# Differential attention scores as one 128-row product, with the high and low parts split before the transposes

## The chip, the cores and the metric

The kernel runs on one core of one Trainium2 chip. The metric is device time in microseconds of one execution. Three runs of the kernel before took 1465.68 us at the median (1465.53 to 1467.9).

## The reference, cut to what matters

Two layers work on 256 latent tokens and 256 context tokens of 1024 channels. In each layer a normalised and modulated stream `h` is projected to the queries, keys and values of four attention branches (2-D neighbourhood "na", differential "df", grouped query "gq", latent "ml"). Each branch's output goes through its own projection, is weighted by a sigmoid gate and added up; an output projection and a gated MLP follow. In layer 0 the context tokens do all of this too; in layer 1 they give only keys and values.

The differential branch has 4 heads with 2 maps each of 32 channels, so 8 groups of 32 for the queries and 8 for the keys. It normalises each group (RMS and a gain), rotates the latent tokens' groups, and computes

```
sc = einsum("bqhmd,bthmd->bhmqt", q, k) * scale      # d = 32, 8 products per token pair
pr = softmax(sc)
a  = pr[:, :, 0] - lam * pr[:, :, 1]
o  = einsum("bhqt,bthd->bqhd", a, v)
```

## The kernel before, in words

All products of the large matrices are done in a rounded 32-bit format (`F32R`) with both operands split into a high and a low part, `x = hi + lo`: `hi*hi + lo*hi + hi*lo`, three matmuls (`mm3`, lines 277 to 280). Weights arrive on SyncE's queue into one of four raw tiles (`wload`, line 267), ScalarE writes the high part and VectorE the low one.

A layer first makes na's keys and values, then its queries. After that come four stages, each given to `drive` (line 282), which emits the steps of several generators in turn, in proportion to the weight that stands beside each. The stage of na's attention carries the projection of df's keys, values and queries; the stage of df's attention carries the gate product of na (`merge`) and gq's projection; and so on for gq and ml. The tile framework then puts the instructions of each engine into an order of its own by a simulated timeline, so an instruction can stand far from where the code emits it. Each engine runs its own list in that order, and semaphores hold what must wait.

A projection (`win_block`, line 442) works on halves of 256 tokens. For a query or key half, `use_qk` (line 636) copies the result from PSUM, normalises it, lets GpSimd rotate it if the tokens are latent, and puts one step `put` on a list, `later`, from which `due` takes one step at a time.

For branches in `SPLIT` (df in layer 0; na, df and gq in layer 1) `put` calls `to_ST` (line 600). It does four 128x128 transposes into one PSUM tile `tp`, and then for each of the four 32-row groups of df a ScalarE copy that rounds to the high part (for queries a second copy of it into another 32 rows) and a VectorE subtraction for the low part. So a key half takes 4 ScalarE and 4 VectorE instructions of 32 rows by 512, a query half 8 and 4. In context halves the gain is applied in these instructions. The result has, per group, 64 rows of the key tile with the high and the low part, 64 rows of the query tile with the high part twice, and the query's low part in a third place. df has 7 such halves: keys and queries of both token sets in layer 0 (4), keys of both and queries of the latent tokens in layer 1 (3).

The score of one map for 128 queries is then two matmuls (`head_scores`, lines 768 and 769): 64 rows for `q_hi*(k_hi + k_lo)` and 32 rows for `q_lo*k_hi`. There are 48 df scores: 16 with 512 keys and 16 with 256 in layer 0, 16 with 512 in layer 1. The same two lines serve na and gq in layer 1, with 128 and 64 rows there. After them `softmax` (line 772) runs on VectorE and ScalarE, and the probabilities are transposed (line 827) and multiplied with the values (line 835).

Keys and queries lie in tiles `kT` (or `kS`) and `qT` (or `qS`); na and gq share one buffer and df and ml another. ml's two small weight matrices and its two intermediate tiles lie in a pool of their own, `mp`. `mla_weights` (line 665) puts their two DMAs on SyncE's queue. `stage()` (line 577) gives a staging tile from a pool of three.

Of the kernel before, what the change touches and what calls it, by code (L numbers as in the profile page):

```python
# [10 lines left out]
F32 = mybir.dt.float32  # L11
F32R = mybir.dt.float32r
AF = mybir.ActivationFunctionType
ALU = mybir.AluOpType
# [217 lines left out]
def backbone(ctx: ExitStack, tc, wb, xT, cc, cb, sm, rg, bias, cst, out):  # L232
# [17 lines left out]
    def spool(es, name, bufs, **k):  # L250
        return es.enter_context(tc.tile_pool(name=name, bufs=bufs, reuse_waits="tile", **k))
# [230 lines left out]
    for l in range(L):  # L482
# [34 lines left out]
        yes = ExitStack()  # L517
        aes = ExitStack()
        qp = spool(aes, f"q{l}", 2)
        stp = spool(aes, f"st{l}", 3)  # L520
        rp = spool(aes, f"rp{l}", 1)


# [16 lines left out]
        kT, qT, Vt = {}, {}, {}  # L540

        split = SPLIT[l]
        nbig = 2 if "na" in split else 1

        def newkq(key):

            if nbig == 1 and key in ("na", "gq"):
                kT[key] = qp.tile([P, 2, T], F32, name="kT", bufs=1)
                qT[key] = qp.tile([P, 2, TT], F32, name="qT", bufs=1)
            else:  # L550
                kT[key] = qp.tile([P, 4, T], F32, name="kS", bufs=nbig)
                qT[key] = qp.tile([P, 6, TT], F32, name="qS", bufs=nbig)
            if key in split:
                kT[key], qT[key] = kT[key].bitcast(F32R), qT[key].bitcast(F32R)
            if key == "ml":
                for i in range(2):
                    kT["ml%d" % i], qT["ml%d" % i] = kT["ml"][:, 2 * i:2 * i + 2], qT["ml"][:, 2 * i:2 * i + 2]

# [41 lines left out]
        def to_ST(dst, src, scale, d, isq):  # L600
# [9 lines left out]
            for r in range(P // d):  # L610
# [10 lines left out]
                else:  # L621
                    stt(lo, tp[rs], g, hi[rs].bitcast(F32), ALU.mult, ALU.subtract)

        def cols(j):
            return slice(256 * j, 256 * j + 256)

        def tcols(t0, na):
            return slice(P * t0, P * (t0 + na))
# [7 lines left out]
        def use_qk(dst, key, h, d, mul, add, gain, tab=None, which=None, e=A):  # L636

            def f(t0, na, ps):
                n = h * d
                st = stage()[:, :na, :n]  # L640
                A.copy(st, ps[:, :, :n])
                r = head_rstd((v4(st, h), mul, add))
                tt(V, v4(st, h), v4(st, h), bc4(r, na, h, d), ALU.mult)
                g = gain
                if tab is not None and t0 < 2:
                    s2 = stage()[:, :na, :n]
                    rope(v4(s2, h), v4(st, h), tab, which, t0)
                    st, g = s2, None
                z = dst[key][:, :, tcols(t0, na)]

                def put():
                    if key in split:
                        to_ST((z[:, :4], z[:, 4:6]) if dst is qT else (z,), st, g, d, dst is qT)
                    else:
                        to_T(z[:, :n // P], st, g, e)
                return [put]
            return f
# [5 lines left out]
        mw = {}  # L663

        def mla_weights():
            mw["kv"] = mp.tile([P, 512], F32, name="wkv")
            nc.sync.dma_start(out=mw["kv"], in_=wb[l, KIDX["kvb",], :, :512])
            mw["q"] = mp.tile([P, 2, 384], F32, name="wq")
            nc.sync.dma_start(out=mw["q"][:96], in_=wb[l, KIDX["qb",], :96, :768].rearrange("p (k n) -> p k n", k=2))

        def use_mkv(t0, na, ps):
            st = stage()
            A.copy(st[:, :, 0:160], ps[:, :, 0:160])
            a, krn = st[:, :, 0:128], st[:, :, 128:160]
            r = head_rstd((a.unsqueeze(2), 1.0 / 128, EPS), (krn.unsqueeze(2), 1.0 / 32, EPS))
            tt(V, a, a, r[:, 0:2].unsqueeze(2).to_broadcast([P, 2, 128]), ALU.mult)
            tt(V, krn, krn, r[:, 2:4].unsqueeze(2).to_broadcast([P, 2, 32]), ALU.mult)
            if t0 < 2:
                rope(st[:, :, 160:192].unsqueeze(2), krn.unsqueeze(2), 1, 2, t0)
                krn = st[:, :, 160:192]  # L680
            got = {}

            def put():
                got["ma"] = mp.tile([P, 256], F32, name="mkv")
                to_T(got["ma"].unsqueeze(1), st[:, :, 0:128], vec("kvag"), A)

            def tok(t):
                ma = got["ma"]
                kv = acc_p.tile([P, 512], F32, name="acc")
                mm(kv, lhsT=ma[:, t * P:(t + 1) * P], rhs=mw["kv"], start=True, stop=True)  # L690
                kv4 = kv.rearrange("p (h d) -> p h d", h=4)
                A.copy(Vt["ml"][:, t0 + t].rearrange("p (h d) -> p h d", h=4), kv4[:, :, 64:128])
                skv = stage().rearrange("p a n -> p (a n)")[:, :384].rearrange("p (h d) -> p h d", h=4)
                kn = skv[:, :, 0:64]
                A.copy(kn, kv4[:, :, 0:64])
                r = head_rstd((kn.unsqueeze(1), 1.0 / 64, EPS))
                tt(V, kn, kn, r.unsqueeze(2).to_broadcast([P, 4, 64]), ALU.mult)
                G.tensor_copy(skv[:, :, 64:96], krn[:, t].unsqueeze(1).to_broadcast([P, 4, 32]))
                got[t] = lambda: mla_T(kT, skv, t0 + t, vec("mkc" if t0 else "mkx", 0, 96), A)

            return [put, lambda: tok(0), lambda: tok(1), lambda: got[0](), lambda: got[1]()]
# [8 lines left out]
        def use_mqa(t0, na, ps):  # L710
# [6 lines left out]
            def put():  # L717
                tp = tp_p.tile([P, 4, P], F32, name="tp")
                for i in range(2):
                    for a in range(2):  # L720
                        nc.tensor.transpose(tp[:96, 2 * i + a], st[:, a, 96 * i:96 * i + 96], ident)
                got["ma"] = mp.tile([P, 2, 256], F32, name="mqa")
                for i in range(2):
                    A.mul(got["ma"][:96, i], tp[:96, 2 * i:2 * i + 2].rearrange("p a t -> p (a t)"), vec("qag", i, 96))

# [31 lines left out]
        def head_scores(key, qs, qt, d, i, r, ik):  # L757
# [4 lines left out]
            n = T if qs == 0 else CL  # L762
            sps = sc_p.tile([P, T], F32, name="sc")
            c = qs * S + qt * P
            ro = r // 2 * 2 * d
            rs, r1 = slice(ro, ro + 2 * d), slice(r * d, r * d + d)
            kk = k[:, 2 * ik + r % 2, T - n:]
# [177 lines left out]
        rt = lay.tile([P, 2, 2, 2, RW], F32, name="rt", bufs=1)  # L945
        rgt = tmp.tile([P, 4, RW], F32, name="t")
        nc.sync.dma_start(out=rgt, in_=rg[l].rearrange("p (a w) -> p a w", a=4))
        rtab0 = tmp.tile([P, 2, 2, RW], F32, name="t")
        nc.sync.dma_start(out=rtab0, in_=cst[:, 512:].rearrange("p (a q w) -> p a q w", a=2, q=2))
        for j in range(2):  # L950
# [9 lines left out]
        y = yp.tile([P, KD, TT], F32, name="y")  # L960
        pp = spool(aes, f"p{l}", 3)
        ptp = spool(aes, f"pt{l}", 3)
        mp = spool(aes, f"mp{l}", 1)
        use_nk = use_qk(kT, "na", 4, 64, *b64, gna)
        for t in range(4):
            p3 = kv[t].rearrange("p (a n) -> p a n", a=1)
# [10 lines left out]
        drive((attend(PAIR, probs_na, Vt["na"], lambda h: 64 * h, post_plain(O)), na),  # L977
              (chain(win_block(l, "dk", A2, use_qk(kT, "df", 8, 32, *b32, vec("dgk"), 1, 1)),
                     win_block(l, "dv", A2, use_v("df")),
                     win_block(l, "dq", qh, use_qk(qT, "df", 8, 32, *q32, vec("dgq"), 0, 1)), flush()), 12 + nq),  # L980
              *early(3))
        newV("gq"); newkq("gq")
        O1 = newO()
# [201 lines left out]
```

## Time and profile before

| | |
|---|---|
| median of three runs | 1465.68 us |
| profiled execution, own time | 1467.0 us |
| its span | 1465.2 us |
| TensorE busy (matmul) | 1424.0 us, 97% |
| TensorE busy (weight load) | 1193.7 us, 81% |
| VectorE busy | 1053.9 us, 72% |
| ScalarE busy | 665.6 us, 45% |
| GpSimd busy | 203.8 us, 14% |

A row for a matmul gives its start and how long it was in flight. Matmuls are pipelined, so the flights of neighbours overlap, and what a matmul occupies of the engine is read from the distance between starts, not from its duration.

### The profile page before, as it was taken

To read this page: it belongs to the slowest core of one execution; us is meant where nothing else is said; L and a number is where in the kernel's file an instruction comes from. 1 tells how busy PE (TensorE), PEld (TensorE's weight loads), DVE (VectorE), ACT (ScalarE), POOL (GpSimd) and SP (SyncE) were. 2 spreads that over 40 slices of the span, in tenths; PEclk is the share of its full clock that TensorE was granted. 3 is DMA by queue.
4 is the path that set the end of the run, shared out by engine and by line. 5 is a ranking of instruction groups with operands and counts; after the bars stand their busy time and mean duration, and the time that the engine had idled before them with its cause. 6 is when DMAs were issued, how large, how long until landed. Compare 5 with 4: busy or idle time off the path is not lost.

```text
span 1465.2 us, 22330 instructions
## 1 busy us (share of the span) xinstructions
PE 1424.0 (97%) x8526; PEld 1193.7 (81%) x8526; DVE 1053.9 (72%) x1911; ACT 665.6 (45%) x1197; POOL 203.8 (14%) x191
## 2 busy tenths in 40 slices
PE   6999999999999998999999999999999999899999
PEld 3787777777677888888888888898788889899999
DVE  5688676747776547899999653778767575787884
ACT  5445543435333334543244432465646554564662
POOL 0253001223111200000000000043123321000000
PEclk9999999999999999999999999999999999999999
DMA  9522121213233541455797322233223343455553
GB/s 376 195 89 92 44 90 58 94 44 130 82 120 113 189 158 58 158 187 188 224 323 256 116 81 92 94 125 98 82 96 104 106 144 131 137 184 183 188 177 112
DMA packets 57930, 202.19 MB, mean 138 GB/s; under 512 B 6560, under 2 KB 8096, under 8 KB 57184
## 3 DMA queue, kind: packets, MB, share of 16 engines
q1 hardware_dynamic: 57824, 200.77, 40.5%
q8 instruction: 67, 1.10, 0.3%
q14 instruction: 39, 0.32, 0.1%
HBM read 199.69 MB, written 1.05 MB: 137 GB/s over the span
## 4 chain that ended last, share of the span: by engine, by line
PE 93%; issue 2%; DVE 2%; ACT 2%; DMA 1%; POOL 0%; SPq 0%; POOLq 0%; DVEq 0%; ACTq 0%
PE acc L278 26%; PE acc L280 26%; PE acc L279 25%; PE av L835 3%; PE sc L754 3%; PE tp L827 2%; PE sc L769 2%; PE sc L768 2%; DVE wl L257 1%; PE acc L730 1%; DMA mraw<-in_wb_dram 1%; ACT wh L272 1%; PE acc L690 1%; PE tp L372 0%; PE tp L608 0%
## 5 line engine op out<-in xcount | busy, mean ns | idle before, releaser
L272 ACT CAST wh<-raw 128x1024 fp32r<-128x1024 f32 (+1 forms) x272 | 279.6, 1029 | 465.8 <-PE acc L279 381.3
L278 PE MATMUL acc<-hh,wh 128*128 128x256 f32 (+1 forms) x1248 | 422.9, 340 | 7.9 <-ACT hh L424 3.9
L257 DVE TENSOR_TENSOR wl<-raw,wh 128x1024 fp32r<-128x1024 f32 (+1 forms) x272 | 332.3, 1222 | 129.0 <-ACT wh L272 123.3
L280 PE MATMUL acc<-hh,wl 128*128 128x256 f32 (+1 forms) x1248 | 417.9, 335 | 0.0
L279 PE MATMUL acc<-hl,wh 128*128 128x256 f32 (+1 forms) x1248 | 417.2, 335 | 0.0
L278 PEld LDWEIGHTS acc<-hh,wh 128*128 128x128 f32 x1248 | 237.7, 191 | 37.0 <-ACT hh L424 7.0
L280 PEld LDWEIGHTS acc<-hh,wl 128*128 128x128 f32 x1248 | 238.3, 191 | 26.2 <-issue 3.8
L279 PEld LDWEIGHTS acc<-hl,wh 128*128 128x128 f32 x1248 | 238.4, 191 | 25.6 <-issue 3.3
L257 POOL TENSOR_TENSOR r<-v,mhalf 128x4 f32<-128x4 f32 (+3 forms) x59 | 80.9, 1376 | 732.6 <-DVE v L405 450.5
L350 DVE SCALAR_TENSOR_TENSOR junk<-raw,cact 128x1024 bf16<-128x1024 f32 x128 | 157.1, 1227 | 17.0 <-DMA raw<-in_wb_dram 16.4
L278 PE MATMUL acc<-wh,hh 128*128 128x256 f32 (+3 forms) x496 | 149.5, 301 | 5.8 <-ACT hh L424 5.8
L279 PE MATMUL acc<-wl,hh 128*128 128x256 f32 (+3 forms) x496 | 147.5, 297 | 0.0
L280 PE MATMUL acc<-wh,hl 128*128 128x256 f32 (+3 forms) x496 | 145.9, 300 | 0.1
L279 PE MATMUL acc<-al,wh 128*128 128x256 f32 (+1 forms) x370 | 121.5, 328 | 0.0
L278 PE MATMUL acc<-ah,wh 128*128 128x256 f32 (+1 forms) x370 | 121.5, 328 | 0.0
L280 PE MATMUL acc<-ah,wl 128*128 128x256 f32 (+1 forms) x370 | 121.4, 328 | 0.0
L254 DVE SCALAR_TENSOR_TENSOR u<-acc,smt,u 128x255 f32<-128x255 f32 (+1 forms) x184 | 108.9, 594 | 4.1 <-ACT u L1084 2.9
L278 PEld LDWEIGHTS acc<-wh,hh 128*128 128x128 f32 x496 | 95.2, 192 | 15.1 <-ACT hh L424 8.3
L777 ACT ACTIVATE p<-sc,nm 128x512 f32<-128x512 f32 (+1 forms) x120 | 74.2, 619 | 66.9 <-DVE nm L774 39.1
L280 PEld LDWEIGHTS acc<-wh,hl 128*128 128x128 f32 x496 | 95.0, 192 | 9.4 <-issue 4.7
L279 PEld LDWEIGHTS acc<-wl,hh 128*128 128x128 f32 x496 | 95.3, 192 | 6.5 <-issue 4.1
L774 DVE TENSOR_REDUCE nm<-sc 128x1 f32<-128x512 f32 (+1 forms) x120 | 71.1, 598 | 36.5 <-PE sc L769 25.9
(165 smaller groups left out, 2065.7 us busy)
## 6 DMA issues: line engine op xcount, KB each, us to landing
raw<-in_wb_dram SPq DMA_DIRECT2D x328, 512.0 KB, 3.4
mraw<-in_wb_dram SPq DMA_DIRECT2D x16, 512.0 KB, 10.2
raw<-in_wb_dram SPq DMA_DIRECT2D x20, 384.0 KB, 2.9
x<-in_xT_dram SPq DMA_DIRECT2D x2, 1024.0 KB, 6.3
bt<-in_bias_dram SPq DMA_DIRECT2D x8, 256.0 KB, 2.9
xt<-in_xT_dram SPq DMA_DIRECT2D x2, 1024.0 KB, 6.9
raw<-in_wb_dram SPq DMA_DIRECT2D x4, 320.0 KB, 2.8
cact<-in_cb_dram SPq DMA_DIRECT2D x1, 1024.0 KB, 11.4
```

What stands on the lines that cost most here:

```text
L254: return V.scalar_tensor_tensor(out=out, in0=in0, scalar=scalar, in1=in1, op0=op0, op1=op1)
L257: e.tensor_tensor(out=out, in0=a, in1=b, op=op)
L272: A.copy(h[:, :w], r[:, :w])
L278: mm(ps, lhsT=a[0], rhs=b[0], start=first, stop=False)
L279: mm(ps, lhsT=a[0], rhs=b[1], start=False, stop=False)
L280: mm(ps, lhsT=a[1], rhs=b[0], start=False, stop=last)
L350: V.scalar_tensor_tensor(out=junk, in0=r, scalar=1.0, in1=cact[:, st_], op0=ALU.mult, op1=ALU.mult, accum_out=o)
L754: mm(sps[:, :n], lhsT=q[o:o + d, c:c + P], rhs=k[o:o + d, T - n:], start=True, stop=True)
L768: mm(sps[:, :n], lhsT=q[rs, 2 * i + r % 2, c:c + P], rhs=kk[rs], start=True, stop=False)
L774: V.tensor_reduce(out=nm, in_=sps[:, :n], op=ALU.max, axis=AX.X, negate=True)
L777: A.activation(out=p[:, :n], in_=sps[:, :n], func=AF.Exp, bias=nm, accum_out=s)
L835: mm(av[64 * j:64 * j + 64], lhsT=V_[:, 4 - nk + i, vcol(hd):vcol(hd) + 64], rhs=PTs[j][:, i], start=i == 0, stop=i == nk - 1, tile_positi ...
```

## The change

For df alone, the split is made on the normalised tokens before the transposes, on all 128 partitions (tokens). For each block of 128 tokens and 4 groups, ScalarE writes the high part and VectorE the low part, each twice, into one staging tile of 512 columns: for queries per group `hi hi lo lo`, for keys `hi lo hi lo`. Four transposes then give, for each of the 4 groups, 128 rows of 32 channels times 4, and one copy of 128x512 (ScalarE or VectorE in turn) moves them to the key or query tile. A score is then one matmul over 128 rows, which also includes `q_lo*k_lo`. A half has four such blocks; their steps are put on `later` so that a block's transposes come two steps after its split. In context halves the gain is multiplied in by one more VectorE instruction of 128x512 ahead of the split; its values are copied once a layer into `dgt`.

The key tile of df and ml grows to 8 slots (queries to 8), and ml's small weights and intermediates move from the pool `mp` into key slots 4 to 7, which ml does not use. So their DMAs now write a buffer that df's keys occupied. There is one more staging tile, and `drive`'s weight of df's projection goes from 12 to 20.

```diff
-        stp = spool(aes, f"st{l}", 3)
+        stp = spool(aes, f"st{l}", 4)
...
+            if key in split and key != "df":
+                kT[key] = qp.tile([P, 4, T], F32, name="kA", bufs=1)
+                qT[key] = qp.tile([P, 6, TT], F32, name="qA", bufs=1)
+            elif key in ("na", "gq"):
+                kT[key] = qp.tile([P, 2, T], F32, name="kA", bufs=1)
+                qT[key] = qp.tile([P, 2, TT], F32, name="qA", bufs=1)
             else:
+                kT[key] = qp.tile([P, 8, T], F32, name="kB", bufs=1)
+                qT[key] = qp.tile([P, 8, TT], F32, name="qB", bufs=1)
...
+        def to_D(dst, src, i, isq):
+            got = []
+            def parts_():
+                w4 = stage().rearrange("p a n -> p (a n)").bitcast(F32R)
+                w = w4.rearrange("p (g x y d) -> p g x y d", g=4, x=2, y=2)
+                s = src.rearrange("p (g d) -> p g d", g=4).unsqueeze(2).to_broadcast([P, 4, 2, 32])
+                hi, lo = (w[:, :, 0], w[:, :, 1]) if isq else (w[:, :, :, 0], w[:, :, :, 1])
+                A.copy(hi, s)
+                tt(V, lo, s, hi.bitcast(F32), ALU.subtract)
+                got.append(w4.bitcast(F32))
+            def turn():
+                tp = tp_p.tile([P, 4, P], F32, name="tp")
+                for g in range(4):
+                    nc.tensor.transpose(tp[:, g], got[0][:, g * P:(g + 1) * P], ident)
+                evac(A if i else V, dst, tp)
+            return [parts_, turn]
...
+                elif key == "df":
+                    tt(V, v4(st, h), v4(st, h), dgt[:, tab]..., ALU.mult)
...
+                if key == "df":
+                    fs = [to_D(z[:, 4 * i:4 * i + 4, a * P:(a + 1) * P], st[:, a, i * P:(i + 1) * P], i, dst is qT)
+                          for a in range(na) for i in range(2)]
+                    steps = [fs[0][0], fs[1][0]]
+                    for x, y_ in zip(fs, fs[2:]):
+                        steps.append(lambda x=x, y_=y_: (y_[0](), x[1]()))
+                    return steps + [fs[-2][1], fs[-1][1]]
...
         def mla_weights():
-            mw["kv"] = mp.tile([P, 512], F32, name="wkv")
+            room = mlroom[0].rearrange("p a t -> p (a t)")
+            mw["kv"], mw["q"] = room[:, 0:512], room[:, 512:1280]...
+            mw["ka"], mw["qa"] = room[:, 1280:1536], room[:, 1536:2048]...
...
+            if d == 32:
+                mm(sps[:, :n], lhsT=q[:, 4 * i + r, c:c + P], rhs=k[:, 4 * ik + r, T - n:], start=True, stop=True)
+                return sps, n
...
+        dgt = lay.tile([P, 2, 32], F32, name="dgt")
+        A.copy(dgt, rgt.rearrange("p (j s) w -> p j s w", s=2)[:, :, 0, 64:96])
...
-                     win_block(l, "dq", qh, use_qk(qT, "df", 8, 32, *q32, vec("dgq"), 0, 1)), flush()), 12 + nq),
+                     win_block(l, "dq", qh, use_qk(qT, "df", 8, 32, *q32, vec("dgq"), 0, 1)), flush()), 20 + nq),
```

## Rows read from the trace of the kernel before

**Rows 1.** The page's busy times and its chain that ended last, by engine.
```profile
PE 1424.0 (97%) x8526; PEld 1193.7 (81%) x8526; DVE 1053.9 (72%) x1911; ACT 665.6 (45%) x1197; POOL 203.8 (14%) x191
...
PE 93%; issue 2%; DVE 2%; ACT 2%; DMA 1%; POOL 0%; SPq 0%; POOLq 0%; DVEq 0%; ACTq 0%
```

**Rows 2.** Busy time by stretch: us, busy (instructions) of each engine, clock, DMA, GB/s.
```profile
83.00:144.00 61.00, 61.00 (x381) 45.63 (x379) 50.27 (x98) 31.85 (x66) 26.25 (x15) 1.00 0.26 83
144.00:270.00 126.00, 126.00 (x639) 93.25 (x637) 86.89 (x192) 58.29 (x131) 14.90 (x15) 1.00 0.21 66
1028.00:1087.00 59.00, 57.84 (x382) 46.30 (x380) 44.82 (x91) 34.22 (x71) 6.19 (x7) 1.00 0.27 90
1087.00:1180.00 93.00, 90.90 (x673) 78.47 (x673) 59.20 (x119) 49.46 (x104) 34.84 (x42) 1.00 0.31 105
```

**Rows 3.** TensorE's longest waits, 80 to 480 us and 950 to 1240 us.
```profile
PE sc L754 <- ACT p L777: 1.5, 3, 0.7
...
PE sc L768 <- ACT p L777: 0.8, 2, 0.6
```

**Rows 4.** The timeline of TensorE around a df score with 512 keys.
```profile
1044.01 0.28 PE L280 MATMUL acc<-wh,hl 128*128 128x256 f32 x1
1044.22 0.50 PE L768 MATMUL sc<-kS,qS 64*128 64x512 f32 x1
1044.64 0.49 PE L769 MATMUL sc<-kS,qS 32*128 32x512 f32 x1
1045.07 0.39 PE L278 MATMUL acc<-wh,hh 128*128 128x256 f32 x1
1045.29 0.28 PE L279 MATMUL acc<-wl,hh 128*128 128x256 f32 x1
```

**Rows 5.** The same around a df score with 256 keys.
```profile
198.14 0.28 PE L279 MATMUL acc<-wl,hh 128*128 128x256 f32 x1
198.35 0.39 PE L768 MATMUL sc<-kS,qS 64*128 64x256 f32 x1
...
199.19 0.28 PE L278 MATMUL acc<-wh,hh 128*128 128x256 f32 x1
```

**Rows 6.** The same where a 128-row score of na runs alone.
```profile
993.46 0.39 PE L768 MATMUL sc<-kS,qS 128*128 128x512 f32 x1
993.69 0.49 PE L827 MATMUL tp<-C,p 128*128 128x128 f32 x3
```

**Rows 7.** The same around four transposes of `to_ST`.
```profile
1006.30 0.28 PE L279 MATMUL acc<-wl,hh 128*128 128x256 f32 x1
1006.42 0.60 PE L608 MATMUL tp<-C,st 128*128 128x128 f32 x4
...
1006.98 0.28 PE L278 MATMUL acc<-wh,hh 128*128 128x256 f32 x1
```

**Rows 8.** Groups by line and form, whole span: count, busy us, mean ns, idle before.
```profile
L583 ACT COPY PT<-tp 128x512 f32<-128x512 f32 x32 | 18.7, 584 | 24.1 <-PE tp L827 24.1
...
L583 ACT CAST qS<-tp 32x512 fp32r<-32x512 f32 x16 | 9.2, 577 | 5.0 <-DVE qS L257 2.5 <-PE tp L608 2.3
L257 DVE TENSOR_TENSOR al<-u,ah 128x256 fp32r<-128x256 f32 x22 | 9.2, 416 | 0.0
...
L1097 ACT CAST ah<-u 128x256 fp32r<-128x256 f32 x22 | 8.7, 394 | 1.0 <-DVE u L257 1.0
...
L608 PE MATMUL tp<-C,st 128*128 128x128 f32 x48 | 7.8, 274 | 0.0
...
L257 DVE TENSOR_TENSOR qS<-tp,qS 32x512 fp32r<-32x512 f32 x8 | 5.5, 685 | 2.7 <-ACT qS L583 2.5
```

**Rows 9.** The DMA of ml's weights; layer 0's last df score and ml's first product.
```profile
L667 SPq DMA_DIRECT2D wkv<-in_wb_dram x2: 327/376/424, 49.8 to 807.4; - x2
...
265.88 0.38 PE L768 MATMUL sc<-kS,qS 64*128 64x256 f32 x1
...
289.19 1.02 PE L690 MATMUL acc<-wkv,mkv 128*128 128x512 f32 x2
```

More of the change, by code (lines that the diff above doesn't have):

```diff
@@ L542, in backbone @@
         split = SPLIT[l]
-        nbig = 2 if "na" in split else 1
+        mlroom = []
         def newkq(key):
-            if nbig == 1 and key in ("na", "gq"):
-                kT[key] = qp.tile([P, 2, T], F32, name="kT", bufs=1)
-                qT[key] = qp.tile([P, 2, TT], F32, name="qT", bufs=1)
-            else:
-                kT[key] = qp.tile([P, 4, T], F32, name="kS", bufs=nbig)
-                qT[key] = qp.tile([P, 6, TT], F32, name="qS", bufs=nbig)
+            if key in split and key != "df":
[4 more added lines that the diff above has]
+                qT[key] = qp.tile([P, 2, TT], F32, name="qA", bufs=1)
+            else:
+                kT[key] = qp.tile([P, 8, T], F32, name="kB", bufs=1)
+                qT[key] = qp.tile([P, 8, TT], F32, name="qB", bufs=1)
             if key in split:
@@ L555, in newkq @@
             if key == "ml":
+                mlroom[:] = [kT["ml"][:, 4:8]]
                 for i in range(2):
@@ L648, in f @@
                     st, g = s2, None
+                elif key == "df":
+                    tt(V, v4(st, h), v4(st, h), dgt[:, tab].unsqueeze(1).unsqueeze(1).to_broadcast([P, na, h, d]), ALU.mult)
                 z = dst[key][:, :, tcols(t0, na)]
+                if key == "df":
[5 more added lines that the diff above has]
+                    return steps + [fs[-2][1], fs[-1][1]]
                 def put():
@@ L665, in mla_weights @@
         def mla_weights():
-            mw["kv"] = mp.tile([P, 512], F32, name="wkv")
+            room = mlroom[0].rearrange("p a t -> p (a t)")
+            mw["kv"], mw["q"] = room[:, 0:512], room[:, 512:1280].rearrange("p (k n) -> p k n", k=2)
+            mw["ka"], mw["qa"] = room[:, 1280:1536], room[:, 1536:2048].rearrange("p (k n) -> p k n", k=2)
             nc.sync.dma_start(out=mw["kv"], in_=wb[l, KIDX["kvb",], :, :512])
-            mw["q"] = mp.tile([P, 2, 384], F32, name="wq")
             nc.sync.dma_start(out=mw["q"][:96], in_=wb[l, KIDX["qb",], :96, :768].rearrange("p (k n) -> p k n", k=2))
@@ L683, in put @@
             def put():
-                got["ma"] = mp.tile([P, 256], F32, name="mkv")
+                got["ma"] = mw["ka"]
                 to_T(got["ma"].unsqueeze(1), st[:, :, 0:128], vec("kvag"), A)
@@ L721, in put @@
                         nc.tensor.transpose(tp[:96, 2 * i + a], st[:, a, 96 * i:96 * i + 96], ident)
-                got["ma"] = mp.tile([P, 2, 256], F32, name="mqa")
+                got["ma"] = mw["qa"]
                 for i in range(2):
```

1 line of the change is left out of this document (removed).

## The prediction

> **What bounds the kernel now.** I read the page's busy times first. TensorE is busy 97% of the span and has 93% of the chain that ended last; the reader is to see that no other engine has more than a few per cent of that chain [rows 1]. A busy TensorE can still be one that is idle between close matmuls, so the next views ask whether anything else holds it in the stages that change. In the stretch of na's attention, 83 to 144 us, where df's keys and queries are made, TensorE is busy 61.00 of 61 us although VectorE is busy 82% of it. In the stretch of df's attention of layer 0 it is 126.00 of 126, and in that of layer 1 57.84 of 59, at a granted clock of 1.00, so the clock can give or take nothing here [rows 2]. The waits of TensorE agree: in both attention phases its longest sums are 1.5 and 0.8 us [rows 3]. So TensorE's own list is the bound here, and a change is worth what it takes from that list, as long as the other engines keep up. What each kind of matmul occupies has to be read from distances between starts.
>
> **The scores.** Around a df score with 512 keys the start of the gate matmul ahead and the start of the second gate matmul behind are 45.29 - 44.01 = 1.28 us apart [rows 4]. In between are two gate matmuls of 256 columns, which stand 0.12 us apart where nothing is between them, as the first two starts of [rows 7] do. So the pair of score matmuls occupies 1.28 - 0.24 = 1.04 us. With 256 keys it is 199.19 - 198.14 = 1.05, less 0.24: 0.81 us [rows 5]. That is far more than two streams, since the start before, the pair itself and the start behind are each spread out (0.21, 0.42, 0.43 and 0.22 us instead of 0.12 and about 0.23). The pair changes the rows of the array in use, 128 to 64 to 32 to 128, and at each change the distance grows.
>
> The new score is one matmul of 128 rows, as all its neighbours are. The nearest row is na's 128-row score with 512 keys where its partner does not follow at once: the next start comes 0.23 us later, and it takes the place of no other time [rows 6]. With 256 keys I take the 0.12 us of any 128-row matmul of that size.
>
> Saved: 16 scores with 512 keys in layer 0 and 16 in layer 1, 32 x (1.04 - 0.23) = 25.9 us; 16 with 256, 16 x (0.81 - 0.12) = 11.0 us. Together 36.9 us.
>
> The Trainium skill, page "TensorE: Matmul & The Clock Gate", sections "LDWEIGHTS (loading the stationary operand)" and "Why this matters for your kernels", says that the time goes by columns alone and that a matmul with 32 rows takes as long as one with 128. By it the pair would be two plain streams, and the whole change would come to nothing (third rival). The trace disagrees, 1.04 us for the pair against 0.23 for one.
>
> **The transposes.** Four transposes of `to_ST` between gate matmuls: 6.98 - 6.30 = 0.68 us, less 0.24, is 0.44 us [rows 7]. A half had one such group and gets four, so 3 x 7 halves = 21 more groups: 9.2 us. They are of the same shape and format, so I take this as it stands. Most of it falls in the stretch before df's attention, where TensorE is already full, so all of it counts. What the trace doesn't show is a group that waits for its data or for a free PSUM tile: the old transposes of this line had no idle time before them in 48 instructions [rows 8]. From below the wait is zero; it may even free something, since one PSUM tile was held through 8 to 12 instructions a half and is now held by one copy. From above it is the second rival's. I take zero.
>
> TensorE in sum: -36.9 + 9.2 = -27.7 us.
>
> **ScalarE and VectorE.** Before, a key half took 4 x 0.577 = 2.31 us of ScalarE and a query half 4.62; either took 4 x 0.685 = 2.74 us of VectorE [rows 8]. Now a half takes four copies of 128x256, which I put at the SBUF cast of that size, 0.394, and two PSUM copies of 128x512 at 0.584: 2.74 us of ScalarE; and four subtractions at 0.416 and two PSUM copies, which I put at the 0.685 us of a VectorE instruction of 512 elements from PSUM: 3.03 us [rows 8]. The three context halves add a multiplication of 512 elements, 0.69 us again. Over 7 halves ScalarE gives 4 x 2.31 + 3 x 4.62 - 7 x 2.74 = 3.9 us back, VectorE takes 7 x 0.29 + 3 x 0.69 = 4.1 us more. Beside TensorE's list both are hidden where VectorE stays at 82%, which the first stretch of [rows 2] bears. The doubled writes read their source with a stride of zero, which no row shows; even at twice the price, the seven halves would cost VectorE 28 x 0.42 = 11.6 us, spread over three stages.
>
> What is late next is VectorE in df's own stage. In layer 0 that stretch loses 24.0 us on TensorE and gets about one half's transposes, 126 to about 103; VectorE's 86.9 plus 1 is then 85%. In layer 1 it goes from 59 to about 47 us, against 44.8 us of VectorE: 95%. At the 82% that is seen to cost nothing the first would need 107 us and the second 55, so at most 4 + 8 = 12 us would come back if no work moved. The stretch after layer 1's has VectorE at 59.2 of 93 us, 64% [rows 2], and the framework orders across stages, so some of it will move. The ends are 0 and 12; I take 4.
>
> **The rest.** The DMAs of ml's weights were issued at 49.8 us in layer 0 [rows 9]. Now they can only go after df's last score, at 265.88, with ml's first product at 289.19 [rows 9], so there are 23 us for a load. Behind a waiting DMA on SyncE's queue are the weight loads of the next stage; four raw tiles, each 24 matmuls of 0.23 us, last TensorE 22 us in layer 0. I cost it at nothing; without that cover it is a few us once a layer. `dgt` is one small ScalarE copy a layer, behind a table that GpSimd's rotations need anyway. The fourth staging tile and the weight of 20 follow the number of steps and add no work.
>
> **The sum.** Profiled execution 1467.0 - 27.7 + 4 = 1443.3 us. The median of the three runs is 1.3 us under the profiled one, so 1442.0.
>
> **The rivals.**
> *VectorE becomes the bound in df's stages.* All 12 us come back: 1450. For it: 95% in layer 1, and each df score has a chain of reduction, exponential, reciprocal and two combinations on VectorE and ScalarE. Against: the waits of [rows 3] are short with 82%, and merge work stands beside it.
> *The new groups stall TensorE: slower.* TensorE runs its list in order. If a group of transposes stands at the head before its split is done, everything behind waits: copy 0.39, subtraction 0.42, and one earlier PSUM copy on each engine, 0.58 and 0.69, make 2.1 us at worst. It decides from 27.7 / 28 groups = 1.0 us each. At 1.5 us, 28 x 1.5 = 42 us, and the time is 1442 - 4 + 42 = 1480. For it: the split is new work just ahead of its transposes, for latent halves behind GpSimd's rotation. Against: the old transposes waited for that rotation too, and had no idle time [rows 8]; two steps lie between.
> *The distance around a score is not due to the rows.* If it came from the write to a fresh score tile, or of the reader behind, it would stay, and only one plain stream a score would go: 32 x 0.23 + 16 x 0.12 = 9.3 us, against 9.2 us of transposes: 1465.7, no change. Against it is [rows 6]. The page named above would give the same time.
> *SyncE's queue is held by ml's weights,* loads come late by some 5 us a layer: 1450.
>
> **How the numbers follow.** Forecast 0.66, VectorE 0.20, stalled groups 0.07, no row effect 0.04, SyncE 0.03. A measurement of this kernel tells about 0.2% (3 us) from no change. Faster: 0.66 + 0.20 + 0.03 = 0.89; within: 0.04; slower: 0.07. The range: its low end is the full 27.7 us with nothing back, 1438, and 4 us less for PSUM tiles that come free sooner and ScalarE's 3.9 us: 1434. Its high end takes in the VectorE rival with the doubled writes at twice their price for half their sum, 1456.
>
> **What would show it.** Right: one score row of 128 rows, with 0.23 and 0.12 us to the next start; TensorE's busy time about 28 us lower with its waits in the attention phases still a few us; the stage of na longer by some 4 us, that of df shorter by 23 in layer 0 and 12 in layer 1; VectorE's share in these above 82%. Wrong: idle time before the transposes of the new groups, or before the df scores behind `p` or `nm`; a weight load that comes late behind ml's.

## The result and the profile after

Four runs of the changed kernel took 1450.45 us at the median (1446.25 to 1452.14), beside 1465.66 us of the kernel before on the same chip: ratio 0.9885, 95% interval 0.9871 to 0.9899. The forecast was 1442.0, its range 1434 to 1456. The gain is 15.2 us where 23.7 were forecast. The profiled execution is the fastest of the four, 1446.25 us with a span of 1444.1. Its granted clock, the mean share of TensorE's full clock, is 0.994; the other three have 0.989 to 0.992. The profiled execution of the kernel before has 0.994, too, so between these two the change is worth 20.8 us (1467.0 against 1446.25) at the same clock.

The page's busy times and its chain by engine answer to [rows 1]. In all rows PE is TensorE, PEld its weight loads, DVE VectorE, ACT ScalarE, POOL GpSimd and SP SyncE:

```profile
PE 1401.8 (97%) x8562; PEld 1191.2 (82%) x8562; DVE 1047.4 (73%) x1928; ACT 657.8 (46%) x1201; POOL 203.5 (14%) x191
...
PE 91%; DVE 3%; issue 2%; ACT 2%; POOL 1%; DMA 1%; SPq 0%; POOLq 0%; DVEq 0%; ACTq 0%
```

TensorE is still the bound, with 22.2 us less work instead of 27.7. The four stretches of [rows 2], with their borders moved to the same events, show where:

```profile
82.00:158.00 76.00, 76.00 (x477) 59.35 (x476) 57.34 (x116) 34.02 (x77) 26.79 (x15) 1.00 0.26 87
158.00:255.00 97.00, 95.27 (x558) 76.58 (x556) 77.68 (x184) 49.72 (x119) 16.07 (x15) 1.00 0.24 81
1014.00:1065.00 51.00, 49.81 (x386) 45.06 (x387) 43.56 (x90) 30.70 (x67) 5.87 (x7) 1.00 0.29 101
1065.00:1157.00 92.00, 89.79 (x669) 77.79 (x668) 59.51 (x120) 50.84 (x105) 35.78 (x42) 1.00 0.34 113
```

Layer 0's two stretches went from 61 + 126 to 76 + 97 us, layer 1's last two from 59 + 93 to 51 + 92. Borders shift when the list is ordered anew, so sums over a whole attention phase say more: from na's first score of a layer to ml's first score. Their rows (stretch; us; busy time of TensorE and the others, with the number of instructions; the last three columns are granted clock, DMA share and GB/s), first before, then after:

```profile
83.60:370.50 286.90, 284.42 (x1526) 210.17 (x1525) 203.30 (x431) 133.69 (x297) 68.69 (x64) 1.00 0.24 78
984.20:1179.50 195.30, 191.23 (x1363) 161.73 (x1362) 139.88 (x268) 110.53 (x222) 60.04 (x62) 1.00 0.31 101
```

```profile
82.10:357.60 275.50, 271.80 (x1557) 210.14 (x1556) 200.92 (x445) 127.76 (x297) 70.69 (x64) 1.00 0.26 87
967.40:1157.40 190.00, 184.60 (x1383) 161.89 (x1382) 138.25 (x275) 107.61 (x224) 60.86 (x62) 1.00 0.31 107
```

The phases give 11.4 and 5.3 us, 16.7 together, at a granted clock of 1.00 on both sides. TensorE's busy time in them fell by 12.6 and 6.6; its idle time rose from 2.5 to 3.7 and from 4.1 to 5.4. These two lengths are the measure for the experiments. The rest of the 21.1 us between the two spans lies outside: 1.5 ahead of the first score, 3.9 between the phases, and 1.0 given back behind them. One thing moved across a border: ahead of the first score TensorE has 428 matmuls after and 447 before. The 19 are projection matmuls of 256 columns, which the new order puts into layer 0's phase, 19 x 0.12 = 2.3 us.

The prices taken from the list hold. TensorE's timeline after the change, around a group of transposes and a score of either size ([rows 4, 5, 7]):

```profile
128.57 0.28 PE L279 MATMUL acc<-wl,hh 128*128 128x256 f32 x1
128.69 0.60 PE L647 MATMUL tp<-C,st 128*128 128x128 f32 x4
129.05 0.36 PE L280 MATMUL acc<-wh,hl 128*128 128x256 f32 x1
129.25 0.28 PE L278 MATMUL acc<-wh,hh 128*128 128x256 f32 x1
...
173.49 0.28 PE L278 MATMUL acc<-wh,hh 128*128 128x256 f32 x1
173.61 0.39 PE L804 MATMUL sc<-kB,qB 128*128 128x512 f32 x1
173.84 0.28 PE L279 MATMUL acc<-wl,hh 128*128 128x256 f32 x1
...
183.78 0.28 PE L804 MATMUL sc<-kB,qB 128*128 128x256 f32 x1
183.90 0.28 PE L279 MATMUL acc<-wl,hh 128*128 128x256 f32 x1
```

A score of 512 keys occupies 173.84 - 173.61 = 0.23 us and one of 256 occupies 0.12, as forecast; the four transposes 129.25 - 128.57 - 0.24 = 0.44, as forecast. TensorE's waits in layer 1's phase answer to [rows 3]:

```profile
PE tp L647 <- DVE kB L593: 1.8, 1, 1.8
PE acc L768 <- ACT kB L762: 0.8, 1, 0.8
```

The first wait is new.

### The profile page after: what moved, and what is told of

Read it like the earlier page. It is cut to its first block, busy times and chain, and to the rows that moved or that the text cites. A ratio compares the mean times of both kernels' runs of the same rounds, so it can differ in the third digit from the quotient of the medians.

```text
span 1444.1 us, 22450 instructions
## 1 busy us (share of the span) xinstructions
PE 1401.8 (97%) x8562; PEld 1191.2 (82%) x8562; DVE 1047.4 (73%) x1928; ACT 657.8 (46%) x1201; POOL 203.5 (14%) x191
## 4 chain that ended last, share of the span: by engine, by line
PE 91%; DVE 3%; issue 2%; ACT 2%; POOL 1%; DMA 1%; SPq 0%; POOLq 0%; DVEq 0%; ACTq 0%
PE acc L278 26%; PE acc L279 26%; PE acc L280 25%; PE av L876 3%; PE sc L792 3%; PE tp L868 2%; DVE wl L257 1%; ACT wh L272 1%; PE tp L647 1%; PE sc L804 1%; PE acc L768 1%; DMA mraw<-in_wb_dram 1%; PE acc L728 1%; PE tp L372 0%; POOL st L257 0%
## 5 line engine op out<-in xcount | busy, mean ns | idle before, releaser
L280 PEld LDWEIGHTS acc<-hh,wl 128*128 128x128 f32 x1248 | 238.5, 191 | 23.7 <-issue 1.6
L257 POOL TENSOR_TENSOR y<-y,t 128x512 f32<-128x512 f32 (+1 forms) x48 | 57.3, 1199 | 217.5 <-DVE t L254 185.2
## 6 DMA issues: line engine op xcount, KB each, us to landing
cact<-in_cb_dram SPq DMA_DIRECT2D x1, 1024.0 KB, 11.4
```

The source lines that it names most:

```text
L257: e.tensor_tensor(out=out, in0=a, in1=b, op=op)
L280: mm(ps, lhsT=a[1], rhs=b[0], start=False, stop=last)
```

## The experiments

Before each result stands what was expected of it. Ratios are to the kernel before on the same chip; "phases" are the two lengths above, 275.5 and 190.0 us for the changed kernel.

**The changed kernel again, unaltered.**

> The changed kernel once more, unaltered, for the spread of its time and for a second trace. Its four runs had granted clocks of 0.994, 0.990, 0.992 and 0.989 and spans of 1444.1, 1448.6, 1448.0 and 1450.0 us. Theory 1 (the spread is TensorE's clock, and the median holds about 4 us of it): times from 1446 to 1452 us that rise as the clock falls, and in the trace more half-clock stretches than in the first one if the clock is below 0.994, with the attention stages unchanged (first score to first latent score 275.5 us in layer 0, 190.0 us in layer 1, within 1 us). Theory 2 (the order of work differs from run to run, in waits for DMAs or semaphores): the attention stages themselves differ by some us at the same clock.

1450.59 us (1448.42 to 1452.58), ratio 0.9886 [0.9869, 0.9903]; phases 275.5 and 190.0, the same to a tenth. The executions differ outside the phases. Both traces have a wait of 2.76 us before the first product on layer 1's normalised tokens (for the copies of line 424); what the clock does at its end differs. Four us in which work has begun again, in the kernel before (whose wait is 2.76 us too), in the changed kernel's profiled execution, and in this one (the last three columns are clock, DMA share, GB/s):

```profile
942.00:946.00 4.00, 4.00 (x14) 3.17 (x13) 3.95 (x11) 2.30 (x5) 0.88 (x1) 0.71 0.02 6
```

```profile
926.00:930.00 4.00, 4.00 (x19) 3.29 (x20) 4.00 (x12) 2.37 (x6) 0.86 (x1) 1.00 0.02 8
```

```profile
926.00:930.00 4.00, 4.00 (x13) 3.32 (x12) 3.34 (x10) 1.96 (x5) 0.86 (x1) 0.50 0.12 49
```

In this run the clock was at the lower level, 1.2 GHz, from the end of the wait on, and TensorE did 13 matmuls where the profiled execution did 19 at the full 2.4 GHz. The time between the phases is 612.9 us here and 609.8 there, 3.1 us longer; behind layer 1's phase this execution is 1.2 us shorter, and its span is 2.1 us longer in all (1446.2 against 1444.1).

**The score in two products again**, on the new tiles: the score's saving by itself.

```diff
-                mm(sps[:, :n], lhsT=q[:, 4 * i + r, c:c + P], rhs=k[:, 4 * ik + r, T - n:], start=True, stop=True)
+                kk = k[:, 4 * ik + r, T - n:]
+                mm(sps[:, :n], lhsT=q[:64, 4 * i + r, c:c + P], rhs=kk[:64], start=True, stop=False)
+                mm(sps[:, :n], lhsT=q[64:96, 4 * i + r, c:c + P], rhs=kk[64:96], start=False, stop=True)
```

> The changed kernel with its score taken back to two matmuls, 64 rows (high query part with both key parts) and 32 rows (low query part with the high key part) of the same new tiles. All else is as changed. It measures the first term of the sum alone, which the prediction put at 36.9 us. Theory 1 (every pair costs what it costs between gate matmuls): about 37 us slower than the changed kernel, 24 us of it between the first score and the first latent score of layer 0, 13 us in layer 1: about 1487 us. Theory 2 (a pair that stands beside transposes or value products shares its switches of rows with them, so the mean pair is cheaper): 31 us slower, 18 of it in layer 0, 12 to 13 in layer 1: about 1481 us. Theory 3 (the score pairs were hidden by VectorE's softmax, what was saved is mostly returned): 20 us or less.

1479.68 us (1477.8 to 1483.21), ratio 1.0093 [1.0073, 1.0113]. So without the merged score the change makes the kernel slower, and the merged score is worth 29.1 us. The phases:

```profile
82.30:377.40 295.10, 292.41 (x1589) 216.49 (x1588) 204.54 (x445) 128.04 (x297) 70.15 (x64) 1.00 0.24 81
989.70:1189.50 199.80, 195.19 (x1400) 165.21 (x1399) 138.84 (x275) 107.61 (x224) 59.74 (x62) 1.00 0.31 102
```

19.6 and 9.8 us longer than after. TensorE's busy time is 20.6 and 10.6 higher, 31.2; with one product 1.8 us of it come back as idle time (5.4 + 3.7 against 4.6 + 2.7 us). Against the kernel before, the same two rows price the preparation (the split, the transposes and the copies): 295.1 - 286.9 = 8.2 and 199.8 - 195.3 = 4.5, together 12.7 us. In this are the 2.3 us of projection matmuls that moved into the phase here, too, so the preparation itself is 10.4 us.

**One transpose a block instead of four**, its result copied into all four groups (the scores are then of other values).

```diff
-                for g in range(4):
-                    nc.tensor.transpose(tp[:, g], got[0][:, g * P:(g + 1) * P], ident)
-                evac(A if i else V, dst, tp)
+                nc.tensor.transpose(tp[:, 0], got[0][:, :P], ident)
+                evac(A if i else V, dst, tp[:, 0:1].to_broadcast([P, 4, P]))
```

> The changed kernel with one transpose for a block in place of four; the copy out of PSUM spreads it over the same 4 x 128 columns, so three of every four groups' data are left out of the result. All 28 copies and all splits stay. It measures the second term of the sum, which the prediction put at 9.2 us. Theory 1 (transposes cost their 0.11 us each and nothing waits): 84 x 0.109 = 9.2 us faster, 1441 us. Theory 2 (in layer 1 TensorE also waits for the copies out of the two PSUM tiles, 1.85 and about 1.3 us at four places in the trace of the changed kernel): 9 us faster and those waits stay or grow, since the copies come at the same pace and the transposes ahead of them are fewer. Theory 3 (the waits come from the number of transposes): 12 us or more faster, with the waits gone.

1445.23 us (1444.33 to 1448.59), ratio 0.9854 [0.9837, 0.9872]. The phases, 272.1 and 190.0:

```profile
83.30:355.40 272.10, 266.05 (x1510) 205.14 (x1509) 201.44 (x445) 127.78 (x297) 70.58 (x64) 1.00 0.27 87
969.90:1159.90 190.00, 182.99 (x1346) 158.85 (x1346) 137.97 (x275) 107.27 (x224) 60.66 (x62) 0.99 0.32 107
```

Busy time fell by 5.75 and 1.61 us, against 21 x 0.44 = 9.2 taken out, and idle time rose by 2.35 and 1.61. Layer 1's phase is also disturbed by the clock, which was at the lower level for 3.4 us in it:

```profile
1001.90:1005.30 3.40, 3.11 (x14) 1.96 (x16) 3.08 (x9) 2.20 (x6) 1.23 (x1) 0.50 0.06 22
```

Half of these 3.11 busy us, about 1.6, is what the clock cost, an estimate. Without it the phases would be some 5.0 us shorter than after, and the busy time some 8.9 us lower, close to the 9.2. About 4 us came back as waits. So from this level on a microsecond off TensorE's list is no longer a microsecond off the phase. No theory had it so.

**96 rows instead of 128**, without `q_lo*k_lo`.

```diff
-                mm(sps[:, :n], lhsT=q[:, 4 * i + r, c:c + P], rhs=k[:, 4 * ik + r, T - n:], start=True, stop=True)
+                mm(sps[:, :n], lhsT=q[:96, 4 * i + r, c:c + P], rhs=k[:96, 4 * ik + r, T - n:], start=True, stop=True)
```

> The changed kernel with a score of 96 rows (high-high, high-low, low-high) in place of 128; the low-low product is left out, so it computes what the kernel before computed. Theory 1 (any number of rows that differs from the 128 of the neighbours costs a switch at both ends, as 64 and 32 rows did: the pair's 1.04 us is two streams of 0.23 and three switches of about 0.2): 48 scores x 0.4 = 19 us slower, 1469 us. Theory 2 (96 rows use the same row groups as 128, as the latent branch's 96-row scores seem to do, 0.43 us each for their two passes without more): no change within 3 us, and the title's 128 rows is a matter of convenience.

1446.5 us (1445.06 to 1451.54), ratio 0.9865 [0.9843, 0.9887]; phases the same within 0.2 us, and from the first na score to the last ml score of layer 0 365.2 us in both. A score in this trace:

```profile
173.49 0.28 PE L278 MATMUL acc<-wh,hh 128*128 128x256 f32 x1
173.61 0.40 PE L804 MATMUL sc<-kB,qB 96*128 96x512 f32 x1
173.84 0.28 PE L279 MATMUL acc<-wl,hh 128*128 128x256 f32 x1
```

Its distances are 0.12 and 0.23 us, as with 128 rows. A matmul of 96 rows between others of 128 pays no change of rows; one of 64 or 32 does.

**All 28 copies of the new groups on ScalarE**, one execution.

```diff
-evac(A if i else V, dst, tp)
+evac(A, dst, tp)
```

> The changed kernel with all 28 copies of the new groups from PSUM on ScalarE (0.58 us each), none on VectorE (0.69 us). In the trace of the changed kernel TensorE waits 1.85 us once and about 0.6 us twice in layer 1 for a PSUM tile that VectorE still has to empty. First score to first latent score takes 275.5 us in layer 0 and 190.0 us in layer 1 in both traces of the changed kernel, so one trace is enough. Theory 1 (the wait is for VectorE's place in its list): layer 1 gets 2 to 3 us shorter, with TensorE's waits for VectorE's key copies gone. Theory 2 (with two PSUM tiles any engine's copies make the same wait): within 1 us, the waits now on ScalarE, which also holds the exponentials.

1445.09 us; phases 274.4 and 188.8. In layer 1 TensorE's idle time falls from 5.40 to 3.99 and the 1.8 us wait is gone: the theory of the copies queued on VectorE is right in kind, at 1.2 us instead of the 2 to 3 expected.

**Less VectorE work**: the scaling of the second map's probabilities left out, 24 instructions of VectorE, about 12 us.

```diff
-            V.tensor_scalar(out=p1[:, :n], in0=p1[:, :n], scalar1=r1, scalar2=None, op0=ALU.mult)
```

> The changed kernel without the scaling of the second map's probabilities in the differential branch (24 VectorE instructions, about 12 us in all, 8 us of it in layer 0), so its result leaves the factor lambda and that map's normalisation out. It asks whether VectorE holds TensorE back since the change: with three of four new transposes gone only 3.5 of 9.2 us came back in the two attention phases, and TensorE's idle time in them rose by 3.9 us. Theory 1 (VectorE's list or the chain of a softmax co-limits): layer 0 (275.5 us) and layer 1 (190.0 us) get shorter by 3 to 6 us together and TensorE's idle time (3.7 and 5.4 us) falls. Theory 2 (TensorE's list alone is the bound; the waits belong to other places): within 1 us.

1447.67 us in one execution; phases 274.5 and 191.4, the second with a stretch of 3.4 us at the lower clock in it (1001.3 to 1004.7 us), which cost about half of that. Taking VectorE work out of df's stages gives 1 us where it could give 12: VectorE's share is not what holds them.

**The second product of na and gq in layer 1 also on 128 rows**, with the query's low part written to both halves.

```diff
-            mm(sps[:, :n], lhsT=q[r1, 4 + i, c:c + P], rhs=kk[r1], start=False, stop=True)
+            mm(sps[:, :n], lhsT=q[:, 4 + 2 * i + r % 2, c:c + P], rhs=kk, start=False, stop=True)
...
```

> The same step for the neighbourhood and grouped-query scores of layer 1: the second matmul of 64 rows becomes one of 128 (the low query part twice, against the high and the low key part). 16 scores; 4 more VectorE instructions of 64x512. By the trace a 128-row and a 64-row matmul together occupy 0.85 us between gate matmuls, two of 128 rows 0.46. Theory 1 (the price between gate matmuls): 16 x 0.39 = 6.2 us faster than the changed kernel. Theory 2 (in place a score saves four fifths of that, as the differential scores did, 29 of 37 us, and VectorE's four instructions of 0.7 us return some): 3 to 5 us faster, 3 to 4 of them between the first score and the first latent score of layer 1. Theory 3 (VectorE co-limits there): within 1 us.

1453.83 us (1447.16 to 1455.19), ratio 0.9896 [0.9872, 0.992]: no gain. Layer 1's phase is 194.2 us, TensorE's idle time in it 10.17. Its longest waits:

```profile
PE tp L648 <- DVE kB L593: 4.1, 2, 2.3
```

The same lesson as with one transpose: the list is reordered, groups of transposes come to the head before VectorE has emptied their PSUM tile, and the saving goes into that. The idle time is 4.8 us above the changed kernel's 5.40. The clock adds to the 194.2 us: it was at the lower level from 1004.1 to 1011.0 and from 1092.9 to 1096.3 us, with 8.4 us of TensorE's busy time in it, half of which, 4.2 us, is the cost, an estimate. The one execution with a granted clock of 0.994 took 1447.16 us, beside 1446.25 for the changed kernel at 0.994: no gain at the same clock either.

**Filler matmuls of 256 columns** into an unused accumulator, five behind the norm's products for the latent tokens and four ahead of them in layer 1's out-projection, so that TensorE has work at its idle places.

```diff
+    def filler(k, w_, x_):
+
+        fz = acc_p.tile([P, T], F32, name="acc")
+        for _ in range(k):
+            mm(fz[:, :256], lhsT=w_, rhs=x_, start=True, stop=True)
...
```

> The changed kernel with small matmuls on unused data put where TensorE stands idle between the last product ahead of a norm and the first behind it (5 of 256 columns behind the row statistics of the latent tokens in each of three places, and 4 more ahead of them in layer 1's output projection); nothing reads what they write. In every trace so far the half-clock stretches begin at these places (near 57, 558, 925 and 1243 us), and the changed kernel's eight runs have granted clocks from 0.989 to 0.994, the kernel before's 0.993 to 0.995. Theory 1 (the clock falls because TensorE is idle there): fewer half-clock stretches behind these places, granted clock 0.995 or more, the median 3 to 6 us below 1450.5 us and the spread smaller. Theory 2 (the matmuls are too few, or the clock falls for another reason): clock and median as before, or up to 4 us slower for the work added.

1468.87 us, ratio 1.0004 [0.9994, 1.0013]; phases 275.6 and 191.5. The fillers moved other work: between the phases the time is 628.8 us instead of 609.8, TensorE's idle time in it 13.0 instead of 5.5, and stretches at the lower clock stayed. So this run says nothing on what the clock is worth.

**The copies on ScalarE, timed; the same with 96 rows; and the changed kernel on that chip.** The edits are those above.

> The changed kernel with the 28 copies on ScalarE, now timed. Its one trace had 274.4 and 188.8 us where the changed kernel has 275.5 and 190.0, none of VectorE's waits before the new transposes, a granted clock of 0.995 and 1445.1 us. Theory 1 (the 1.85 us wait at 998 us sets off a half-clock stretch in some executions: kernels with a wait there show one beginning at 1001 to 1004 us): the clock stays at 0.994 or more, median 1445 to 1447 us, 4 us under the changed kernel on the same chip. Theory 2 (the half-clock stretches come at the layer's ends alone and by chance): the two attention phases give 2.3 us, and the clock is spread from 0.989 to 0.995 as before: median 1448 us.

> The same with scores of 96 rows in place of 128. The 96-row kernel had 1446.5 us at the median, 4 us under the changed kernel, with the same two phases (275.5 and 190.0 us within 0.1) and a clock of 0.995, 0.995, 0.996 and 0.990. Theory 1 (fewer rows at work make no time in themselves, the difference was the clock by chance): the same as the kernel with 128 rows and the copies on ScalarE, within 1.5 us. Theory 2 (96 rows keep the clock up): 2 us or more under it, clock 0.995 or above throughout.

> The changed kernel unaltered, on the same chip as the two others, for the comparison: 1450 to 1451 us at the median, clock 0.989 to 0.994, and 275.5 and 190.0 us in the two attention phases.

Copies on ScalarE: 1445.9 us (1443.95 to 1446.12), ratio 0.9856 [0.9841, 0.9871]. With 96 rows as well: 1445.8 (1443.83 to 1446.11), 0.9855 [0.984, 0.987]. Unaltered: 1450.05 (1445.97 to 1451.04), 0.988 [0.9862, 0.9898]. The phases of the first:

```profile
83.30:357.50 274.20, 270.92 (x1557) 210.34 (x1556) 197.80 (x437) 131.18 (x305) 72.17 (x64) 1.00 0.26 87
969.80:1158.60 188.80, 184.85 (x1384) 161.84 (x1383) 134.56 (x269) 110.14 (x230) 61.72 (x62) 1.00 0.33 108
```

It beats both kernels: 4.15 us under the change as it was at the medians. 1.3 + 1.2 us of that are in the phases. The rest goes with the clock, 0.993 to 0.995 in its four executions against 0.990 to 0.995; where both kernels have 0.995, the times are 1443.95 and 1445.97, 2.0 us apart. The 96 rows add nothing.

**The weight of df's projection back at 12**, one execution.

```diff
-win_block(l, "dq", ...), flush()), 20 + nq),
+win_block(l, "dq", ...), flush()), 12 + nq),
```

> The changed kernel with drive's weight of the differential projection back at 12 (from 20), so its steps are emitted later beside the neighbourhood attention. Theory 1 (the weight only spreads the steps): 275.5 and 190.0 us in the two phases change by less than 1 us. Theory 2 (steps left over behind the attention hold the first differential score back): layer 0 or 1 longer by 2 us or more, with a wait before a differential score or its transposes.

1458.82 us; phases 280.0 and 193.7, 4.5 and 3.7 longer. A new wait of 2.0 us for probabilities on VectorE and a stretch at the lower clock stand inside layer 0's phase, and a second such stretch in layer 1's:

```profile
185.60:192.40 6.80, 5.71 (x22) 3.46 (x22) 5.95 (x17) 1.96 (x7) 0.00 (x0) 0.50 0.47 155
1056.00:1062.80 6.80, 5.98 (x22) 3.27 (x22) 5.67 (x15) 3.26 (x9) 0.00 (x0) 0.50 0.00 0
```

Half of the 11.7 us that TensorE was busy in these two, some 5.8, is the clock's part of the 8.2, an estimate. TensorE's idle time in the phases is 2.6 us above the changed kernel's. So the weight of 20, which the prediction put at nothing, is worth 2.6 us of waits here; whether the clock falls there in every execution one trace can't say.

## Why the prediction was right, and where its sum was not

**The bound.** Right: TensorE's list set the time before and sets it after, 97% of the span, and the gain came from what was taken off it.

**The scores: the term that was mis-sized.** "Together 36.9 us" held in kind (undone, the kernel loses 29.1 us and is slower than before) but was 7.8 us too much. The single distances were right. The multiplication was not: it gave each of the 48 pairs all three of its changes of rows. What a change costs shows in TensorE's weight loads, here around a pair before and around a score after:

```profile
1044.22 0.18 PEld L768 LDWEIGHTS sc<-kS,qS 64*128 64x128 f32 x1
1044.64 0.18 PEld L769 LDWEIGHTS sc<-kS,qS 32*128 32x128 f32 x1 [0.24 <-issue]
1045.07 0.19 PEld L278 LDWEIGHTS acc<-wh,hh 128*128 128x128 f32 x1 [0.24 <-issue]
```

```profile
173.50 0.19 PEld L804 LDWEIGHTS sc<-kB,qB 128*128 128x128 f32 x1
```

The load of the new score starts at 173.50 us, 0.11 ahead of its matmul, while the matmul before it runs. Each of the three loads around the pair starts only with its own matmul (1044.22, 1044.64, 1045.07 in [rows 4]). Over the whole span, wherever TensorE is not idle between two matmuls, that is so at all 310 changes between 128, 64 and 32 rows or columns in the kernel before and at all 186 after (96 counted as 128), but at only 9 of the 7,588 places before where both matmuls have 128 rows and 128 columns. Three changes make (1.04 - 2 x 0.23) / 3 = 0.19 us each.

Not every pair has three of its own. In the two phases of the changed kernel 187 loads start only with their matmul; with two products it is 306, so 119 more and not 3 x 48 = 144. The 25 that are missing are 25 x 0.19 = 4.8 us, an estimate. TensorE's busy time, 31.2 us higher with two products, lacks 5.7 of 36.9, so this is most of it. A further 1.8 came back as idle time. The two make 7.5 of the 7.8.

Two kinds of place make them. One is where two pairs follow each other, at seven places, as here in the kernel before:

```profile
1057.96 0.28 PE L280 MATMUL acc<-wh,hl 128*128 128x256 f32 x1
1058.17 0.49 PE L768 MATMUL sc<-kS,qS 64*128 64x512 f32 x1
1058.59 0.50 PE L769 MATMUL sc<-kS,qS 32*128 32x512 f32 x1
1059.02 0.49 PE L768 MATMUL sc<-kS,qS 64*128 64x512 f32 x1
1059.44 0.50 PE L769 MATMUL sc<-kS,qS 32*128 32x512 f32 x1
1059.87 0.38 PE L278 MATMUL acc<-hh,wh 128*128 128x256 f32 x1
1060.09 0.28 PE L279 MATMUL acc<-hl,wh 128*128 128x256 f32 x1
```

From the start of the matmul ahead to the second behind are 2.13 us, less 0.24 is 1.89, not 2 x 1.04 = 2.08: 0.19 us less for one change shared. The other is at the new scores: at 22 places at or right behind the 48 the load still starts only with its matmul, 11 of them beside the value products, which use 64 of 128 columns, so that a change stands there with one product as well. (7 + 22 is 4 more than 25; in the rest of the new order 4 went away.) A new score behind a value product:

```profile
1021.48 0.50 PE L804 MATMUL sc<-kB,qB 128*128 128x512 f32 x1
1022.01 0.38 PE L278 MATMUL acc<-Oh,wh 128*128 128x256 f32 x1
```

The next start comes 0.50 us later (0.53 less 0.03 of idle time), not 0.23. Only 12 of the 32 pairs with 512 keys and 8 of the 16 with 256 stand between two plain matmuls.

The Trainium skill, page "TensorE: Matmul & The Clock Gate", section "Why this matters for your kernels", says that a single matmul with 32 rows takes as long as one with 128. The runs agree with equal times for 96 and 128 rows and disagree where 128, 64 and 32 rows alternate: there a score's second matmul costs 29.1 us over 48 scores, and plain streams would have cost 9.3.

**The preparation: the second term.** 9.2 us were forecast for the transposes and 4 for VectorE. The transposes are right: with the score in two products the preparation measures 10.4 us, and TensorE's busy time fell by some 8.9 where three of four transposes were taken out. The 4 us for VectorE are not there by their cause: its share in df's own stage became 80% (77.68 of 97) and 85% (43.56 of 51), not 95, since work moved to the stretch before, and with 12 us less work layer 0's phase gained 1. "I take zero" for stalls failed in small: TensorE's idle time in the phases is 2.5 us higher than before. Against the sum, -27.7 and 4, the two profiled executions of the same clock show -22.2 us of busy time and 1.1 us of idle time over the whole span. That the 4 us were too many hid 2.9 of the 5.5 that the list fell short, which is luck.

The stalls are those of the second rival. One of them, in the changed kernel's timeline of TensorE and VectorE (the last bracket is the idle time and what ended it):

```profile
997.48 0.66 PE L647 MATMUL tp<-C,st 128*128 128x128 f32 x4
997.55 1.21 DVE L257 TENSOR_TENSOR wl<-raw,wh 128x1024 fp32r<-128x1024 f32 x1
997.97 0.60 PE L868 MATMUL tp<-C,p 128*128 128x128 f32 x4
998.69 0.41 DVE L257 TENSOR_TENSOR st<-st 128x256 fp32r<-128x256 f32 x1
999.02 0.75 DVE L257 TENSOR_TENSOR sc<-sc,bt 128x256 f32<-128x256 f32 x2
999.69 0.68 DVE L593 CAST kB<-tp 128x512 fp32r<-128x512 f32 x1
1000.42 0.66 PE L647 MATMUL tp<-C,st 128*128 128x128 f32 x4 [1.85 <-DVE kB L593]
```

The copy that empties the group's PSUM tile stands on VectorE behind a weight split, the next block's subtraction and two bias additions, 2.4 us in all. The rival priced one late group at 2.1 us at worst and asked for 1.0 on all 28; the price was near (1.85), the number is one in this phase and none in layer 0's. With the copies on ScalarE the wait is gone and the phases are 2.5 us shorter.

**SyncE's queue.** Costed at nothing, and right: ml's weights go out right behind df's last score, land 4.5 us after their issue, and ml's first product stands at 277.62 us in layer 0. The DMA issues (first and last start), df's last score and that product:

```profile
L707 SPq DMA_DIRECT2D kB<-in_wb_dram x2: 424/424/424, 255.0 to 1065.2; - x2
```

```profile
254.32 0.32 PE L804 MATMUL sc<-kB,qB 128*128 128x256 f32 x1
...
277.62 1.02 PE L728 MATMUL acc<-kB 128*128 128x512 f32 x2
```

No matmul in the phases waits for a DMA. The same weights in a room of their own, with the larger key tiles beside it, were not tried, nor was the fourth staging tile taken away.

**The drive weight.** Costed at nothing, and wrong: with 12 in its place the phases have 2.6 us more of waits, and 8.2 us more in all with the lower clock, in one execution. So the higher weight, which spreads df's projection differently over the stages, helps to keep the stalls of the new work small. It also moved part of the borders: na's stage in layer 0 grew by 15 us instead of 4 and df's shrank by 29 instead of 23, and with 12 the first df score comes at 153.1 us rather than 158.2 (144.6 before).

**The clock.** "The clock can give or take nothing here" holds in the phases and was carried to the whole. The two profiled executions at 0.994 differ by 20.8 us; the medians differ by 15.2. Over 12 executions of the changed kernel the mean granted clock is 0.991, over 29 of the kernel before 0.994, and 0.003 of 1450 us is some 4 us, an estimate. So of the 8.4 us by which the median lies above the forecast, about 5.6 came with the executions at a lower clock and 2.9 from the sum (23.7 forecast, 20.8 at the same clock). Behind the wait of 2.76 us the clock was at the lower level for some 3 us before, and in the changed kernel not at all or for some 7. That executions of one list differ so is shown; why the changed kernel falls to the lower level more often is open. Fewer new waits may matter, since the version with the copies on ScalarE ran at 0.993 to 0.995, but this was not tested by itself.

**The rivals.** VectorE as the bound, the distance without an effect of rows (by it the merged score would have given 9.3 us; it gave 29.1) and SyncE's queue are ruled out. Stalled groups are there, too few to turn the sign.

## What to carry to other kernels

A matmul of 64 or 32 rows between full ones costs by its changes of rows, and a distance measured around one pair overstates the whole where pairs stand together or beside matmuls of other columns: count the changes that go away before multiplying. Adding rows that carry a useless product was free here (96 and 128 rows took the same); what paid was one product that is like its neighbours instead of two that are not. Where work is put ahead of transposes on a list that is 97% full, ask which engine empties their PSUM tile and what stands in its queue, and put the copy on the engine with the shorter one.

## What the runs showed that was not expected

- A change of rows (128 to 64 to 32 to 128) spreads starts to 0.21, 0.42, 0.43 and 0.22 us, and the weight load there starts only with its own matmul; 96 rows beside 128 spread nothing (phases equal within 0.2 us).
- The same list with the same 2.76 us wait is followed by a granted clock of 1.00 in one execution and 0.50 in another, 3.1 us apart between the phases.
- Taking three of four transposes out of each new group, 9.2 us of TensorE, shortened the two phases by 3.4 us, or some 5.0 at the full clock.
